# Order of a unit's maxima and the scaling of the unit ahead of it on VectorE, in a forgetting-attention stage

## The chip, the core and the metric

The kernel runs on one core of a Trainium2 chip. A core has five engines with instruction streams of their own: TensorE (PE; its weight loads are listed as PEld), VectorE (DVE), ScalarE (ACT), GpSimd (POOL) and SyncE (SP, which here issues DMA transfers). Each works through its own stream in order and waits on semaphores that the others raise. The metric is the device time of one execution in microseconds.

## What is computed

Two layers over a residual stream of 512 tokens by 1024 features, in float32: dilated sliding-window attention, a gated convolutional FFN, then forgetting attention with shared keys and values, and another FFN. The change lies in the forgetting attention:

```python
def fox_mixer(xn, w_q, w_o, k, v, c):
    q = (xn @ w_q).reshape(B, T, B_HEADS, HEAD_DIM)
    c_t = c.transpose(0, 2, 1)
    scale = HEAD_DIM ** -0.5
    for i in range(T // BLK):
        q0, q1 = i * BLK, (i + 1) * BLK
        s = jnp.einsum('bqhd,bkhd->bhqk', q[:, q0:q1], k[:, :q1]).astype(jnp.float32) * scale
        s = s + (c_t[:, :, q0:q1, None] - c_t[:, :, None, :q1])
        causal = jnp.arange(q0, q1)[:, None] >= jnp.arange(q1)[None, :]
        s = jnp.where(causal, s, NEG)
        p = jax.nn.softmax(s, axis=-1).astype(v.dtype)
        outs.append(jnp.einsum('bhqk,bkhd->bqhd', p, v[:, :q1]))
    o = jnp.concatenate(outs, axis=1)
    return o.reshape(B, T, B_WIDTH) @ w_o
```

There are 16 heads of 64 features and four blocks of 128 queries; block i sees (i + 1) x 128 keys.

## The kernel before

The program is written out in order for each engine; a library adds the semaphores and hands out buffers from pools (`t4`: ten buffers of 4 KB a partition, shared by raw weights, biases, probabilities and the rows of the cumulative gate; `bank`: eight banks of PSUM). Matrix products are made of three PE passes over operands split into a high and a low part, so that a weight that arrives as float32 goes through a copy on ACT (`W.high`, L57) and a subtraction on DVE (`W.low`, L69). In heads 2 to 5 of the attention the low part is made in another way: ACT writes the negated high part (`W.minus`, L64) and a DMA issued by POOL adds the raw weight to it (`W.low_added`, L84).

"Head" below is a pair of heads, 0 to 7, that share the 128 partitions; "block" is one of the four query blocks. A unit is (head j, block i), 32 in all, and the loop at L1668 runs over n with unit n alive and three rounds of tail. In round n:

- at block 2, PE does a quarter of a query projection (`q_part`), the scores of blocks 2 and 3 of this head and of blocks 0 and 1 of the next one (`f_scores`, L1578, tile `s_ps`), and then the products with the values of the head before (`f_pv`, L1627, tile `o_ps`); at other blocks PE does a quarter of a projection alone, up to head 7. From unit (6,3) on PE also does parts of the output projection (`po.both`, tile `acc`).
- `f_norm` takes the unit before (n - 1): a reciprocal of the row sums (L1598) and, for each of the two heads, a scaling of the probabilities in place (L1600), on DVE.
- `f_exp` takes unit n: for each of the two heads a DVE instruction adds the bias to the scores, writes the sum and keeps the row's extreme (L1588, followed by a read of its accumulator into `nm`), and ACT takes the exponential with the row sum (L1590).
- `f_bias` lets POOL make the bias of unit n + 1: two scalings of the gate's rows (L1560) and a causal select (L1561).
- then, at their blocks, DVE's low part of the query (`q_low`, L1506, block 1), of a weight (L69, block 2 in heads 0 and 1 and in units from (6,2) on), and of the output of the head before (`f_out_low`, L1641, block 3).
- `f_transpose` takes unit n - 2: PE transposes its scaled probabilities (L1612, tile `pT_ps`) and ACT copies them out (L1614).
- at block 1 of heads 2 to 5 come `W.minus` and `W.low_added`; `q_high` (L1500) at block 0, `f_out_high` (L1637) behind the values, `W.high` at one block a head.

The values of a head need the copies of all four of its units; the scores need banks that earlier reductions and copies have released. After the loop come the rest of the output projection, a norm and the last FFN (tile `first` is its first product).

The two functions:

```python
def f_exp(j, i):
    ...
    for hh in range(2):
        dve.tensor_tensor_reduce(p[:, hh, :n], s[hh][:, :n], bias[:, hh, :n], -0.125, BIG, ALU.add, ALU.min,
                                 nm[:, hh:hh + 1])
        act.activation(p[:, hh, :n], p[:, hh, :n], AF.Exp, bias=nm[:, hh:hh + 1], scale=-1.0,
                       accum_out=ls[:, hh:hh + 1])

def f_norm(j, i):
    ...
    dve.reciprocal(rl, ls)
    for hh in range(2):
        dve.tensor_scalar(p[:, hh, :n], p[:, hh, :n], rl[:, hh:hh + 1], None, ALU.mult)
```

Of the kernel before, what the change touches and what calls it, by code (L numbers as in the profile page):

```python
# [103 lines left out]
def trunk_kernel(ctx, tc, x, norm_gains, w_qkv_a, w_o_a, w_q_b, w_o_b, kv_norm, w_kvf, b_f,  # L104
# [14 lines left out]
    def t4(shape, dt=F32, name="t4"):  # L119
        return p4.tile(shape, dt, tag="t4", name=name)  # L120
# [7 lines left out]
    def small(n, name):  # L128
        return sml.tile([128, n], F32, tag=name, name=name)
# [1346 lines left out]
    def load_ck(j):  # L1476
        t = t4([128, 2, T], name="ck")
        s = cd[2 * j:2 * j + 2, :]
        sp.dma_start(t, bass.AP(tensor=s.tensor, offset=s.offset, ap=[[0, 128], [T, 2], [1, T]]))
        cks[j] = t  # L1480
# [4 lines left out]
    def q_part(j, i):  # L1485

        if j >= 8:
            return
        if i == 0:
            qps[j] = (bank([128, T], name="q_ps"), [t.rearrange("p (k c) -> p k c", k=8) for t in W.get()])  # L1490
        o, (wh, wl) = qps[j]
        for kc in (2 * i, 2 * i + 1):
            bh, bl = xs(xTq, kc, ALL)
            mm3(o, wh[:, kc, :], wl[:, kc, :], bh, bl, kc == 0, kc == KD - 1)

    def q_high(j):
        if j >= 8:
            return
        qT[j] = t8([128, 2, T], F32R, name="qst")
        act.copy(qT[j][:, 0], qps[j][0])  # L1500

    def q_low(j):
        if j >= 8:
            return
        o, t = qps.pop(j)[0], qT[j]
        dve.tensor_tensor(t[:, 1], o, t[:, 0].bitcast(F32), ALU.subtract)  # L1506
# [48 lines left out]
    def f_bias(j, i):  # L1555
        n = (i + 1) * 128
        bias = t4([128, 2, T], name="bias")
        for hh in range(2):
            hd = 2 * j + hh
            pool.tensor_scalar(bias[:, hh, :n], cks[j][:, hh, :n], -1.0, cq[:, i, hd:hd + 1], ALU.mult, ALU.add)  # L1560
        pool.affine_select(bias[:, :, n - 128:n], bias[:, :, n - 128:n], pattern=[[0, 2], [-1, 128]],  # L1561
                           compare_op=ALU.is_ge, fill=NEG, base=0, channel_multiplier=1)
        bia[j, i] = bias
# [3 lines left out]
    def f_scores(j, blocks):  # L1567
        wide = blocks[0] >= 2
        if not wide:
            both = [bank([128, 2, 256], name="s_ps") for _ in range(2)]  # L1570
        k = kst[j // 2][:, j % 2]
        for i in blocks:
            nn = max(256, (i + 1) * 128)
            sc[j, i] = [bank([128, T], name="s_ps") for _ in range(2)] if wide else [o[:, i] for o in both]
            for qp, kp in ((0, 0), (0, 1), (1, 0)):
                for hh in range(2):
                    own = slice(64 * hh, 64 * hh + 64)
                    pe.matmul(sc[j, i][hh][:, :nn], qT[j][own, qp, i * 128:(i + 1) * 128], k[own, kp, :nn],  # L1578
                              start=qp + kp == 0, stop=qp == 1)

    def f_exp(j, i):
        n = (i + 1) * 128
        s = sc.pop((j, i))
        bias = bia.pop((j, i))
        p = t4([128, 2, T], name="prob")
        nm, ls = small(2, "nm"), small(2, "ls")
# [5 lines that stand above are left out]
        prob[j, i] = (p, ls)  # L1592

    def f_norm(j, i):
        n = (i + 1) * 128
        p, ls = prob[j, i]
        rl = small(2, "rl")
# [3 lines that stand above are left out]
# [3 lines left out]
    def f_transpose(j, i):  # L1604
        p, _ = prob.pop((j, i))
        for hh in range(2):
            if i >= 2 or hh == 0:
                o = bank([128, 4, 128], name="pT_ps")
                t = t2([128, 4, 128], name="pT")
            k0 = (i + 1) * hh if i < 2 else 0  # L1610
            for k in range(i + 1):
                pe.transpose(o[:, k0 + k, :], p[:, hh, k * 128:(k + 1) * 128], ident)  # L1612
            if i >= 2 or hh == 1:
                act.copy(t[:, :k0 + i + 1], o[:, :k0 + i + 1])  # L1614
            pT[j, i, hh] = t[:, k0:k0 + i + 1]
# [4 lines left out]
    def f_pv(j, i):  # L1620
        if i == 0:
            ops[j] = bank([128, T], name="o_ps")
        o = ops[j]
        for k in range(i + 1):
            for hh in range(2):
                hd = 2 * j + hh
                pe.matmul(o[64 * hh:64 * hh + 64, i * 128:(i + 1) * 128],  # L1627
                          Vt[hd // 8][:, k, (hd % 8) * 64:(hd % 8) * 64 + 64], pT[j, i, hh][:, k, :],
                          start=k == 0, stop=k == i)
        del pT[j, i, 0], pT[j, i, 1]  # L1630

    def f_out_high(j):
        o = ops[j]
        if j % 2 == 0:
            OTb[j // 2] = t8([128, 2, 2, T], F32R, name=f"OTb{j // 2}")
        t = OTb[j // 2]
        act.copy(t[:, 0, j % 2, :], o)  # L1637

    def f_out_low(j):
        o, t = ops.pop(j), OTb[j // 2]  # L1640
        dve.tensor_tensor(t[:, 1, j % 2, :], o, t[:, 0, j % 2, :].bitcast(F32), ALU.subtract)  # L1641
# [16 lines left out]
    def values_of(n):  # L1658
        nonlocal pv_next
        while pv_next < n - 2:  # L1660
            j, i = units[pv_next]
            pv_next += 1
            f_pv(j, i)
            if i == 3:
                outs.append(j)

    f_scores(0, (0, 1))
    for n in range(N + 3):  # L1668
        live = n < N
        if live:  # L1670
            j, i = units[n]
            if i == 0 and j + 1 < 8:
                load_ck(j + 1)
            if i == 2:
                q_part(j + 2, 1)
                f_scores(j, (2, 3))
                if j + 1 < 8:
                    f_scores(j + 1, (0, 1))
                values_of(n)
        if 1 <= n <= N:  # L1680
            f_norm(*units[n - 1])
        if live:
            f_exp(j, i)
            if n + 1 < N:
                f_bias(*units[n + 1])
            if i == 1:
                q_low(j + 1)
            if i == 2 and j < 2 or (j, i) >= (6, 2):
                W.low()
            if i == 3 and j:  # L1690
                f_out_low(j - 1)
            if i != 2:
                q_part(j + 1 + (i > 0), (i + 3) % 4)
            if (j, i) in ((7, 1), (7, 2)):
                next(down1)
        if 2 <= n < N + 2:
            f_transpose(*units[n - 2])
        if live and i == 1 and 2 <= j < 6:
            W.minus()
            W.low_added()  # L1700
        if n >= N + 3 - len(fill):
            po.both(*fill[n - N - 3 + len(fill)])

        if n >= N and n % 4 in (0, 2):
            values_of(n)
        while outs:
            f_out_high(outs.pop())
        if live and i == 0:
            q_high(j + 1)
        if live and (i == (j < 2) if j < 6 else (j, i) >= (6, 1) and W.n_split < wo + 4):  # L1710
            W.high()
# [53 lines left out]
```

## Time and profile before

| what | value |
|---|---|
| median of 3 runs | 1111.93 us (1111.66 to 1112.12) |
| profiled execution, its own time | 1113.65 us |
| its span, first to last instruction | 1111.9 us |
| granted TensorE clock, mean | 0.999 |
| attention loop in the span | about 624 to 732 us |
| DVE, scalings L1600, in all | x64, 30.1 us, mean 511 ns |
| DVE, reductions L1588, in all | x64, 28.5 us, mean 481 ns |
| ACT, exponentials L1590, in all | x64, 35.6 us, mean 561 ns |

The profile is of one execution. A row of the order of time has the start in the span, the duration, engine, line, operation, output and inputs, shapes, the number of instructions merged, and in brackets the idle time just before it with what ended it. In "x2" rows the duration is that of both from the first's start to the second's end; neighbouring instructions overlap a little. Rows of waits read: who waited, for whom, microseconds in total, times, longest. A releaser is inferred from semaphores; where the named engine had long been done, it was another.

### The profile page before, as it was taken

The numbers are of one execution on the slowest core, as the hardware profiler recorded it, in microseconds if no ns is written. First come the engines' busy times: TensorE is split into PE (matmuls) and PEld (weight loads), VectorE is DVE, ScalarE is ACT, GpSimd is POOL, SyncE is SP. The second block draws the span as 40 slices with busy tenths as digits, with TensorE's granted clock in tenths as the row PEclk, the third lists the DMA queues.
The fourth block names the chain that finished last, engine by engine and source line by source line (L and its number), as shares of the span: only waits on it lengthen the run. The fifth ranks groups of instructions, "written<-read, shape, count | busy, mean of one in ns | idle before, by whom it ended". The sixth has DMA issues, their size and how long they took to land. (4 is left out here: it accounts for less than half of the span.)

```text
span 1111.9 us, 18030 instructions
## 1 busy us (share of the span) xinstructions
PE 1100.4 (99%) x6610; PEld 953.5 (86%) x6610; DVE 879.9 (79%) x1484; ACT 660.9 (59%) x1088; POOL 214.0 (19%) x313
## 2 busy tenths in 40 slices
PE   9999999999999999999999999999999999999997
PEld 5988889999999988888878888789999999988886
DVE  6597778888788779997686676868887887779994
ACT  5554566656666747576451487746556665747572
POOL 1823000411111211000000445500411111211000
PEclk9999999999999999999999999999999999999999
DMA  9499864368878989794448444593379788989872
GB/s 324 164 328 408 337 190 126 85 180 200 202 184 189 239 269 326 292 321 115 133 152 280 158 113 115 176 283 112 83 179 213 188 190 193 231 263 319 317 246 76
DMA packets 184242, 236.26 MB, mean 212 GB/s; under 512 B 11673, under 2 KB 131465, under 8 KB 184154
## 3 DMA queue, kind: packets, MB, share of 16 engines
q1 hardware_dynamic: 169210, 182.94, 50.2%
q0 software_dynamic: 14944, 52.18, 20.5%
q8 instruction: 52, 0.85, 0.3%
q14 instruction: 36, 0.29, 0.1%
HBM read 166.08 MB, written 39.63 MB: 185 GB/s over the span
## 5 line engine op out<-in xcount | busy, mean ns | idle before, releaser
L264 PE MATMUL acc<-w 128*128 128x512 f32 (+1 forms) x311 | 120.6, 388 | 0.3 <-DVE mix L326 0.3
L266 PE MATMUL acc<-w 128*128 128x512 f32 (+1 forms) x311 | 120.4, 387 | 0.0
L69 DVE TENSOR_TENSOR w<-wraw,w 128x1024 fp32r<-128x1024 f32 x74 | 97.4, 1332 | 25.6 <-ACT w L57 25.0
L57 ACT CAST w<-wraw 128x1024 fp32r<-128x1024 f32 x94 | 96.8, 1049 | 21.0 <-PE v_ps L265 6.9
L265 PE MATMUL acc<-w 128*128 128x512 f32 (+1 forms) x267 | 103.2, 387 | 0.0
L264 PE MATMUL up<-xsh,w 128*128 128x256 f32 x352 | 99.6, 283 | 0.0
L265 PE MATMUL up<-xsl,w 128*128 128x256 f32 x352 | 99.6, 283 | 0.0
L266 PE MATMUL up<-xsh,w 128*128 128x256 f32 x352 | 99.6, 283 | 0.0
L614 ACT ACTIVATE bb<-up,conv 128x512 f32<-128x512 f32 x80 | 59.6, 775 | 58.4 <-DVE up L1001 47.6
L265 PE MATMUL up<-xbl,w 128*128 128x512 f32 (+1 forms) x276 | 93.5, 339 | 0.0
L265 PE MATMUL up<-xcl,w 128*128 128x512 f32 (+1 forms) x276 | 93.5, 339 | 0.0
L264 PE MATMUL up<-xbh,w 128*128 128x512 f32 (+1 forms) x276 | 93.5, 339 | 0.0
L264 PE MATMUL up<-xch,w 128*128 128x512 f32 (+1 forms) x276 | 93.5, 339 | 0.0
L266 PE MATMUL up<-xbh,w 128*128 128x512 f32 (+1 forms) x276 | 93.4, 338 | 0.0
L266 PE MATMUL up<-xch,w 128*128 128x512 f32 (+1 forms) x276 | 93.4, 338 | 0.0
L264 PEld LDWEIGHTS acc<-w 128*128 128x128 f32 x311 | 58.4, 188 | 12.5 <-DVE mix L326 0.7
L266 PEld LDWEIGHTS acc<-w 128*128 128x128 f32 x311 | 58.4, 188 | 12.0
L264 PEld LDWEIGHTS up<-xsh,w 128*128 128x128 f32 x352 | 67.6, 192 | 0.0
L265 PEld LDWEIGHTS up<-xsl,w 128*128 128x128 f32 x352 | 67.6, 192 | 0.0
L266 PEld LDWEIGHTS up<-xsh,w 128*128 128x128 f32 x352 | 67.6, 192 | 0.0
L615 DVE SCALAR_TENSOR_TENSOR bb<-up,conv,bb 128x511 f32<-128x511 f32 x80 | 59.5, 744 | 5.5 <-ACT bb L614 5.2
L617 DVE SCALAR_TENSOR_TENSOR bb<-up,conv,bb 128x510 f32<-128x510 f32 x80 | 59.9, 749 | 2.8
(313 smaller groups left out, 3123.4 us busy)
## 6 DMA issues: line engine op xcount, KB each, us to landing
wraw<-in_w_up_dram SPq DMA_DIRECT2D x88, 512.0 KB, 6.0
w<-wraw POOLq DMA_DIRECT2D x32, 512.0 KB, 6.3
dT<-dsums SPq DMA_DIRECT2D x28, 512.0 KB, 7.6
w<-wsum POOLq DMA_DIRECT2D x24, 512.0 KB, 5.8
dsums<-in_w_down_dram SPq DMA_DIRECT2D x22, 512.0 KB, 7.6
dsums<-in_w_down_dram SPq DMA_DIRECT2D x44, 256.0 KB, 5.6
hD<-hc POOLq DMA_DIRECT2D x44, 256.0 KB, 6.5
dact<-hD SPq DMA_DIRECT2D x44, 256.0 KB, 5.9
```

Source lines behind the costliest of these rows:

```text
L57: self.nc.scalar.copy(pair[:, 0], raw)
L69: self.nc.vector.tensor_tensor(pair[:, 1], raw, pair[:, 0].bitcast(F32), ALU.subtract)
L264: pe.matmul(o, ah, bh, start=first, stop=False, skip_group_check=shared)
L265: pe.matmul(o, ah, bl, start=False, stop=False, skip_group_check=shared)
L266: pe.matmul(o, al, bh, start=False, stop=last, skip_group_check=shared)
L614: act.activation(bb[:, s, :], ps, AF.Identity, bias=cp[:, 3, ch:ch + 1], scale=cp[:, 2, ch:ch + 1])
L615: dve.scalar_tensor_tensor(bb[:, s, 1:], ps[:, :T - 1], cp[:, 1, ch:ch + 1], bb[:, s, 1:], ALU.mult, ALU.add)
L617: dve.scalar_tensor_tensor(bb[:, s, 2:], ps[:, :T - 2], cp[:, 0, ch:ch + 1], bb[:, s, 2:], ALU.mult, ALU.add)
```

## The change

In each round `f_exp` of the unit alive now comes ahead of `f_norm` of the unit before. Nothing else moves: `f_bias` and what follows keep their places, and in the last rounds, where no unit is alive, `f_norm` stands as it did.

```diff
                 if j + 1 < 8:
                     f_scores(j + 1, (0, 1))
                 values_of(n)
+        if live:
+            f_exp(j, i)
         if 1 <= n <= N:
             f_norm(*units[n - 1])
         if live:
-            f_exp(j, i)
             if n + 1 < N:
                 f_bias(*units[n + 1])
             if i == 1:
```

On DVE the order of one round was: reciprocal and two scalings of unit n - 1, two reductions of unit n. It becomes: two reductions of unit n, reciprocal and two scalings of unit n - 1. ACT's, POOL's, SP's and PE's streams keep their instructions and their order.

## The prediction

> **What bounds the kernel now.** I read the page's busy times first, then TensorE's (PE's) own waits in the attention stage from 618 to 735 us, then the order of time on PE, VectorE (DVE), ScalarE (ACT) and GpSimd (POOL) in that stage.
>
> ```profile
> PE 1100.4 (99%) x6610; PEld 953.5 (86%) x6610; DVE 879.9 (79%) x1484; ACT 660.9 (59%) x1088; POOL 214.0 (19%) x313
> ...
> PE s_ps L1578 <- ACT pT L1614: 1.0, 3, 0.5
> PE pT_ps L1612 <- DVE prob L1600: 0.5, 2, 0.3
> PE acc L264 <- DVE nm L1588: 0.4, 1, 0.4
> PE s_ps L1578 <- DVE nm L1588: 0.3, 1, 0.3
> ```
>
> PE is busy 99% of the span, so the kernel can gain only what PE still waits. The waits listed, with the 0.29 at 717.53 further down, are 2.5 us, all in the stage that the change touches, and all on DVE's reductions and scalings or on ACT's copies behind them. They understate the loss, because PE's row goes on for a while after its last real issue. The scores of a head against the values of the head before it show it better: both blocks have the same work for heads 2 to 6, and each scores block runs until the o_ps block starts.
>
> ```profile
> 652.41 2.21 PE L1578 MATMUL s_ps<-kst,qst 64*128 64x384 f32 x24
> 654.55 2.40 PE L1627 MATMUL o_ps<-pT,Vt 128*64 128x128 f32 x40
> ...
> 664.81 2.42 PE L1578 MATMUL s_ps<-kst,qst 64*128 64x384 f32 x24
> 667.16 2.40 PE L1627 MATMUL o_ps<-pT,Vt 128*64 128x128 f32 x40
> ...
> 677.38 1.61 PE L1578 MATMUL s_ps<-kst,qst 64*128 64x384 f32 x13
> ...
> 680.14 2.40 PE L1627 MATMUL o_ps<-pT,Vt 128*64 128x128 f32 x40
> ...
> 690.37 1.60 PE L1578 MATMUL s_ps<-kst,qst 64*128 64x384 f32 x13
> ...
> 693.09 2.40 PE L1627 MATMUL o_ps<-pT,Vt 128*64 128x128 f32 x40
> ...
> 700.03 1.29 PE L1612 MATMUL pT_ps<-ident,prob 128*128 128x128 f32 x8 [0.27 <-DVE prob L1600]
> 701.25 0.44 PE L1578 MATMUL s_ps<-kst,qst 64*128 64x384 f32 x1
> ...
> 705.20 2.40 PE L1627 MATMUL o_ps<-pT,Vt 128*64 128x128 f32 x40
> ...
> 712.67 1.25 PE L1612 MATMUL pT_ps<-ident,prob 128*128 128x128 f32 x8 [0.22 <-DVE prob L1600]
> ...
> 715.24 2.00 PE L1578 MATMUL s_ps<-kst,qst 64*128 64x384 f32 x12
> 717.53 2.40 PE L1627 MATMUL o_ps<-pT,Vt 128*64 128x128 f32 x40 [0.29 <-ACT pT L1614]
> ```
>
> Start to start, the scores take 2.14 us for head 2 (654.55 - 652.41), then 2.35, 2.76, 2.72 and 3.95 for heads 3 to 6. Against head 2 that is 0.21, 0.62, 0.58 and 1.81 lost. Head 7 has 12 of the 24 matmuls and takes 2.29; the wide half of 2.14 is about 1.3, so about 1.0 is lost. With the idle of the other waits on DVE (0.27 + 0.22 + 0.4) the loss is 5.1 us, my ceiling for what this stage can give. From head 2 to head 3 PE needs 12.40 us (664.81 - 652.41); later heads take 12.57 and 12.99. The loss grows from head to head: something beside PE is a little slower than PE and falls behind.
>
> That something is a ring through four engines. One turn, head 4 to head 5:
>
> ```profile
> 679.55 1.08 ACT L64 ACTIVATE w<-wraw 128x1024 fp32r<-128x1024 f32 x1
> ...
> 680.92 0.89 POOL L84 DMA_DIRECT2D w<-wraw  x1 [4.34 <-ACT w L64]
> ...
> 681.54 1.67 POOL L1560 TENSOR_SCALAR bias<-ck,cq 128x512 f32<-128x512 f32 x2
> ...
> 682.05 1.86 DVE L1600 TENSOR_SCALAR prob<-prob,rl 128x384 f32<-128x384 f32 x2
> ...
> 683.29 0.41 POOL L1561 TENSOR_SCALAR_AFFINE_SELECT bias<-bias 128x256 f32<-128x256 f32 x1
> ...
> 683.83 0.68 DVE L1588 CUSTOM_DVE_ANT_0 prob<-s_ps,bias 128x512 f32<-128x512 f32 x1
> ...
> 685.05 0.68 DVE L1641 TENSOR_TENSOR OTb<-o_ps,OTb 128x512 fp32r<-128x512 f32 x1
> ...
> 686.11 0.17 DVE L1598 RECIPROCAL rl<-ls 128x2 f32<-128x2 f32 x1 [0.37 <-ACT prob L1590]
> ...
> 686.31 1.02 DVE L1600 TENSOR_SCALAR prob<-prob,rl 128x512 f32<-128x512 f32 x2
> 687.25 0.28 DVE L1588 CUSTOM_DVE_ANT_0 prob<-s_ps,bias 128x128 f32<-128x128 f32 x1
> ...
> 687.62 0.40 ACT L1590 ACTIVATE prob<-prob,nm 128x128 f32<-128x128 f32 x1 [1.08 <-DVE nm L1588]
> ...
> 692.50 1.08 ACT L64 ACTIVATE w<-wraw 128x1024 fp32r<-128x1024 f32 x1
> ```
>
> ACT's negated weight (L64) releases POOL's accumulating DMA; behind that in POOL's order comes the bias of block 3, which the reduction of block 3 needs; then DVE's low part of the output (L1641), the exponential of block 3 awaited, its scaling, the reduction of the next head's block 0; then ACT's exponential, copies, a weight, and L64 again. In steps: 1.37 + 0.62 + 2.29 (681.54 to 683.83) + 1.22 + 2.20 (685.05 to 687.25) + 0.37 + 4.88 (687.62 to 692.50) = 12.95. PE needs 12.40. The ring loses 0.55 a head until PE waits for it.
>
> **The change part by part.** It removes and adds no instruction. In each of 31 units the two reductions (L1588, with their accumulator reads) and, on ACT, the two exponentials come ahead of the reciprocal and two scalings (L1598, L1600) of the unit before. No DMA is issued by either step; only DVE's order changes, and POOL, SP, ACT and PE keep theirs. So DVE's busy time stays, but three things change on the ring.
>
> First, the wait for the exponential goes. Today the step of 2.20 holds that wait and the scaling of block 3; afterwards the reduction of the next block 0 follows L1641 without either. What comes into the ring is the scaling of block 2, today done beside POOL's bias, afterwards queued behind the reduction of block 3, which waits for that bias. Its price has two ends:
>
> ```profile
> 636.47 0.88 DVE L1600 TENSOR_SCALAR prob<-prob,rl 128x512 f32<-128x512 f32 x2
> ...
> 640.02 1.36 POOL L1560 TENSOR_SCALAR bias<-ck,cq 128x512 f32<-128x512 f32 x2 [3.96 <-DVE nm L1588]
> ...
> 644.27 0.75 DVE L1600 TENSOR_SCALAR prob<-prob,rl 128x384 f32<-128x384 f32 x2
> ...
> 648.72 0.40 ACT L1590 ACTIVATE prob<-prob,nm 128x128 f32<-128x128 f32 x1 [0.99 <-ACT pT L1614]
> ...
> 685.23 0.94 POOL L1560 TENSOR_SCALAR bias<-ck,cq 128x256 f32<-128x256 f32 x2 [0.25 <-DVE nm L1588]
> ```
>
> Alone the two scalings of 384 take 0.75; beside POOL's bias of 512 they took 1.86, that is 1.11 more. In the new place POOL works on the bias of 256 (0.47 a piece), which starts as soon as the reduction of block 3 is done, just when the scaling starts. The nearest row for one blocked piece is the 1.11 beside pieces of 0.83; by size that is 0.63, so I take 1.38, between 0.75 and 1.86. The ring's 2.20 becomes 0.20 (reciprocal, 686.11 to 686.31) + 0.75 to 1.86 + 0.62 (L1641) = 1.57 to 2.68, taken 2.20: the same. Second, the bias of block 3 no longer runs beside a scaling: 1.36 for 1.67, 0.31 less. So a turn takes 12.0 to 13.1, taken 12.6: 0.2 a head behind PE in place of 0.55.
>
> Third, the ring starts earlier. The row at 648.72 shows ACT idle for 0.99 before the first exponential of head 2, waiting (the releaser named was long done) for the reduction that stood behind a scaling; that goes. The start of L64 after the first score of its head is 2.17 for head 4 (679.55 - 677.38); head 2 is two turns of about 0.5 earlier, 1.2. Afterwards 0.2 for head 2 and 0.2 more a head, 0.8 at head 5. Head 2 loses nothing at 1.2, head 3 0.21 at 1.7; so heads 3 to 5 lose nothing: 0.21 + 0.62 + 0.58 = 1.41 gained.
>
> What is late next is the scaling itself. It was ahead of the reduction and is now behind it, so PE's transposes of that unit (one unit later in PE's order) may wait.
>
> ```profile
> 662.46 1.04 PE L1612 MATMUL pT_ps<-ident,prob 128*128 128x128 f32 x8
> ```
>
> For blocks 0 to 2 a projection step or the values (2.4) lie between; hidden. Block 3 is scaled after the next head's first reduction: 1.37 + 0.62 + 1.98 + 1.22 + 2.20 = 7.4 after L64 that reduction starts, two halves take 0.4, the reciprocal 0.2, and the first half of the scaling 0.44 (0.88 / 2) alone or 1.0 behind a blocked piece of 0.6; taken 8.8. PE gets there 10.1 after the first score of an undisturbed head (662.46 - 652.41), and with L64 0.2 to 0.6 after that score the scaling is through at 9.0 to 9.4: hidden. In head 5 PE has no projection step left to put between and gets there at 8.8 (700.03 - 0.27 - 690.37 - 0.58); the scaling is through at 0.8 + 8.8 = 9.6, so PE waits 0.8 where it waits 0.27 now: 0.5 lost. If the cover went in every head, it would be rival (c).
>
> Head 6: scores wait today for copies and reductions that the ring delivers late (1.81). With the ring 1.4 earlier against PE, the last copy of head 5 ends before the values want it: 1.8 gained. Heads 6 and 7 then load DVE with three low parts of weights. Between the first reduction of (6,2) and the scaling of (6,3) DVE then also does the scaling of (6,1), 0.2 + 0.5 (two thirds of 0.75), and the reduction of (7,0), 0.4: 1.1 more. It starts earlier by what the ring has gained on PE, 1.3 at head 5 (2.13 to 0.8), of which head 5's longer wait at its transposes takes back 0.5: net 0.3 later. Waits of 0.4 + 0.22 become about 0.8 to 0.9: 0.2 lost. By head 7's scores this DVE work is through, and the copy that PE waits for there has no idle ACT before it: 1.0 gained.
>
> Sum: 1.4 + 1.8 + 1.0 - 0.5 - 0.2 = 3.5, and 0.3 for the earlier start of what comes after a wait (the idle of 0.27, 0.22 and 0.4 leaves out PE's refill): 3.8 us. The profiled execution took 1113.65 with a span of 1111.9, so 1.75 lies around the span; it would take 1109.85. The runs shown have a median of 1111.93, so 1108.1.
>
> Does the gain survive to the end?
>
> ```profile
> 745.20 1.05 ACT L57 CAST w<-wraw 128x1024 fp32r<-128x1024 f32 x1 [0.85 <-DMA wraw<-in_w_up_dram]
> ...
> 766.68 0.28 PE L264 MATMUL first<-xch,w 128*128 128x256 f32 x1
> ...
> PE acc L264 <- DVE mix L326: 0.3, 1, 0.3
> ```
>
> The fourth up-weight of the last FFN has its high part at 746.3, 20 us before the first product; and from 735 us to the end PE waits once, 0.3 us. PE simply arrives earlier.
>
> By the Trainium skill, page "SBUF — State Buffer", section "Who interferes with whom", a DVE instruction in a two-port mode and a GpSimd instruction exclude each other for the whole instruction, and whichever starts first wins. The rows agree (1.86 beside POOL, 0.75 alone). This speaks against the change, since each reduction now releases a bias on POOL at the moment that a scaling starts; it is the first rival.
>
> **The rivals.** (a) Every scaling that meets a bias waits for a whole piece each time: 0.47 twice for block 2, so the ring is 12.0 + 0.94 = 12.9, as slow as today, and only the head start of 1.0 is left: L64 comes 0.2, 0.7, 1.3 and 1.8 after the first score of heads 2 to 5, and head 5 loses 0.3 in its scores. Block 3's scaling meets the bias of 384 (a piece lies between 0.47 for 256 and 0.68 for 512, say 0.58), and its first half is through 9.3 after L64, so at 9.5, 10.0, 10.6 and 11.1 against 10.1 and, in head 5, 8.8: PE waits 0.5 in head 4 and, the ring having gained on PE by these 0.8, 1.5 in head 5. From 3.8 come off 0.3 + 0.5 + 0.7 (1.5 for 0.8): 2.3 gained, 1109.6. For it: 1.86. Against it: the scaling at 686.31 ran beside POOL's work and took 1.02 against 0.88 alone.
>
> (b) The change does not do what it says: the waits of PE go but others of the same size stand behind them (buffers freed by transposes that are now later, DMA in the last stage), 1111.9. For it: the ring's other steps (12.95 - 2.20) are untouched. Against it: the 20 us above.
>
> (c) Slower: the scaling becomes the slow member. Its place is between the reduction of block 3 and PE's transposes; its price is the full 1.86 in the ring, 13.1 a turn, and 0.2 for the landing of the accumulating DMA, whose raw weight's buffer the next probabilities take. PE is then paced at 13.3 instead of 12.40, 12.57 and 12.99: 39.9 - 38.0 = 1.9 over three heads and 0.5 in head 5, 2.4 in all: 1114.3. It decides from a ring of 12.7 (38.0 / 3) on, once the head start of 1.0 is used up. Against it: 12.6 is my middle. For it: each full block costs 1.1 a head.
>
> **How the numbers follow.** Chances: forecast 0.62, (a) 0.18, (b) 0.11, (c) 0.09. What a measurement can tell from no change is about 0.2%, 2.2 us: below 1109.7 is faster, above 1114.1 slower. Faster: 0.62 x 0.97 + half of (a), which lies on the bound = 0.69; slower 0.08, most of (c); the rest, 0.23, is within. The range reaches down to the ceiling with refill, 5.1 + 0.6 = 5.7 gained, 1106.2, and up past (a) to the lower edge of (b), 1111.7, which leaves out (c) and half of (b). The forecast's own range is 1106.2 to 1109.5.
>
> **What would show it.** On DVE each L1588 pair stands before L1598, and ACT's idle before block 0's exponential (1.08, 0.99) is gone. The scores of heads 3 to 6 take about 2.14 up to the o_ps row. PE's waits on L1600 stay or grow at the transposes of (5,3) and (6,3); waits on L1614 vanish. L64 comes every 12.4 to 12.6 us. The prediction is wrong if L1600 beside POOL takes 1.9 in the new place as a rule, if PE waits on prob L1600 in heads 2 to 4, or if new waits arise after 735 us.

## The result, and the profile after

The changed kernel takes 1110.51 us (median of 15 runs, 1109.56 to 1111.58) beside 1112.24 for the kernel before (15 runs): a ratio of 0.9982, 95% interval 0.9974 to 0.999, so 1.1 to 2.9 us less. A second comparison (E9 below) gave 0.9979, 0.9969 to 0.999. The forecast was 1108.1, a gain of 3.8, in a range from 1106.2 to 1111.7. The gains of the two comparisons, 1.7 and 2.7 us, lie near rival (a)'s 2.3; the time is inside the range, but above the forecast's own 1106.2 to 1109.5.

The two profiled executions differ by more, 1113.65 and 1109.58, but not all of that is the change. PE's clock on five rows of the order of time, before and after, columns as in the prediction:

```profile
624.62 0.97 PE L1578 MATMUL s_ps<-kst,qst 64*128 64x256 f32 x12
...
642.16 2.40 PE L1627 MATMUL o_ps<-pT,Vt 128*64 128x128 f32 x40
...
730.08 1.75 PE L1627 MATMUL o_ps<-pT,Vt 128*64 128x128 f32 x28
```

```profile
623.16 0.98 PE L1578 MATMUL s_ps<-kst,qst 64*128 64x256 f32 x12
...
641.31 2.40 PE L1627 MATMUL o_ps<-pT,Vt 128*64 128x128 f32 x40
...
651.56 2.21 PE L1578 MATMUL s_ps<-kst,qst 64*128 64x384 f32 x24
653.71 2.40 PE L1627 MATMUL o_ps<-pT,Vt 128*64 128x128 f32 x40
...
688.67 2.21 PE L1578 MATMUL s_ps<-kst,qst 64*128 64x384 f32 x24
690.82 2.40 PE L1627 MATMUL o_ps<-pT,Vt 128*64 128x128 f32 x40
...
697.65 1.29 PE L1612 MATMUL pT_ps<-ident,prob 128*128 128x128 f32 x8 [0.16 <-ACT prob L1590]
698.87 2.62 PE L1578 MATMUL s_ps<-kst,qst 64*128 64x384 f32 x24
701.42 2.40 PE L1627 MATMUL o_ps<-pT,Vt 128*64 128x128 f32 x40
...
709.14 0.66 PE L1612 MATMUL pT_ps<-ident,prob 128*128 128x128 f32 x4 [1.08 <-DVE prob L1600]
...
712.02 1.49 PE L1578 MATMUL s_ps<-kst,qst 64*128 64x384 f32 x12
713.44 2.40 PE L1627 MATMUL o_ps<-pT,Vt 128*64 128x128 f32 x40
...
725.98 1.75 PE L1627 MATMUL o_ps<-pT,Vt 128*64 128x128 f32 x28
```

PE is 1.46 us earlier at the first score already, ahead of the first changed instruction; that belongs to the start of the program in that one execution of before, where PE waits 1.0 and 0.3 us (`qk_ps`) that it does not wait after. In the fourteen profiles of this document the first score lies between 622.97 and 624.62. From the first score (first row) to the last values (last row) the stage takes 105.5 us before and 102.8 after, 2.6 less, which lies inside the intervals of the runs. This stage time is the measure used below. What lies behind it is 381.8 us in both, and there PE's one wait is the one of before (`acc <- DVE mix`, 0.3): nothing is given back later. It is 381.8 in the other runs too, but for E6 (382.3) and E7 (382.0), where a weight load of the last FFN waits 0.7 and 0.4 for a landing.

PE's waits after, all of the stage (who, for whom, us, times, longest):

```profile
PE pT_ps L1612 <- DVE prob L1600: 1.5, 3, 1.1
...
PE pT_ps L1612 <- ACT pT L1614: 0.3, 1, 0.3
PE pT_ps L1612 <- ACT prob L1590: 0.2, 1, 0.2
```

The waits of the scores on copies (1.0) and those on the reductions (0.4 and 0.3) are gone, and PE now waits longer for scalings, 1.5 for 0.5. The same ring as in the prediction, head 4 to head 5, after:

```profile
677.03 1.08 ACT L64 ACTIVATE w<-wraw 128x1024 fp32r<-128x1024 f32 x1
...
678.41 0.89 POOL L84 DMA_DIRECT2D w<-wraw  x1 [3.96 <-ACT w L64]
678.42 2.44 DVE L1600 TENSOR_SCALAR prob<-prob,rl 128x256 f32<-128x256 f32 x2
...
679.03 1.67 POOL L1560 TENSOR_SCALAR bias<-ck,cq 128x512 f32<-128x512 f32 x2
...
681.22 0.69 DVE L1588 CUSTOM_DVE_ANT_0 prob<-s_ps,bias 128x512 f32<-128x512 f32 x1 [0.36 <-POOL bias L1561]
...
682.63 1.25 POOL L1560 TENSOR_SCALAR bias<-ck,cq 128x256 f32<-128x256 f32 x2 [0.25 <-DVE rl L1598]
...
682.64 0.90 DVE L1600 TENSOR_SCALAR prob<-prob,rl 128x384 f32<-128x384 f32 x2
...
683.47 0.67 DVE L1641 TENSOR_TENSOR OTb<-o_ps,OTb 128x512 fp32r<-128x512 f32 x1
...
684.06 0.28 DVE L1588 CUSTOM_DVE_ANT_0 prob<-s_ps,bias 128x128 f32<-128x128 f32 x1
...
684.43 0.41 ACT L1590 ACTIVATE prob<-prob,nm 128x128 f32<-128x128 f32 x1 [0.41 <-DVE nm L1588]
...
689.32 1.09 ACT L64 ACTIVATE w<-wraw 128x1024 fp32r<-128x1024 f32 x1
```

A turn is 12.29 us here, 12.95 before. ACT's idle ahead of block 0's exponential is 0.41, 1.08 before. The scaling of block 2 stands in the ring now and takes 0.90; beside it POOL's pieces for 256 keys take 1.25 where they took 0.94.

### The profile page after: what moved, and what is told of

It is laid out like the page before. It is cut to its first block, busy times and chain, and to the rows that moved or that the text cites. A ratio compares the mean times of both kernels' runs of the same rounds, so it can differ in the third digit from the quotient of the medians.

```text
span 1107.8 us, 18033 instructions
## 1 busy us (share of the span) xinstructions
PE 1097.9 (99%) x6610; PEld 952.7 (86%) x6610; DVE 880.1 (79%) x1484; ACT 661.2 (60%) x1088; POOL 218.8 (20%) x313
## 4 chain that ended last, share of the span: by engine, by line
PE 94%; DVE 2%; ACT 2%; DMA 1%; issue 1%; POOL 0%; DVEq 0%; ACTq 0%; POOLq 0%
PE up L266 13%; PE up L265 13%; PE up L264 13%; PE acc L264 8%; PE acc L266 8%; PE acc L265 8%; PE v_ps L264 2%; PE v_ps L266 2%; PE v_ps L265 2%; PE qk_ps L265 2%; PE qk_ps L264 2%; PE qk_ps L266 2%; PE first L264 1%; PE first L266 1%; PE first L265 1%; PE k_ps L264 1%
```

## The experiments

All runs at a glance; "stage" is from the profile of the run, worked out from unrounded times. The medians of before beside them are 1112.58 (E1 to E4), 1113.11 (E5 to E8) and 1112.5 (E9 to E12).

| run | order of maxima and scaling | median us | ratio to before, 95% | stage us |
|---|---|---|---|---|
| before | old | 1112.24 | | 105.47 |
| changed | new | 1110.51 | 0.9982, 0.9974 to 0.999 | 102.81 |
| E1 | new at block 0 alone | 1109.65 | 0.9974, 0.9962 to 0.9985 | 103.25 |
| E2 | new at block 3 alone | 1113.86 | 1.001, 1.0001 to 1.002 | 106.53 |
| E3 | old in round 3 | 1109.76 | 0.9975, 0.9965 to 0.9984 | 103.45 |
| E4 | old in round 28 | 1108.93 | 0.9973, 0.9963 to 0.9984 | 102.25 |
| E5 | old in rounds 3 and 28 | 1109.98 | 0.9972, 0.9962 to 0.9982 | 101.69 |
| E6 | new, buffers exchanged | 1109.55 | 0.9971, 0.996 to 0.9982 | 102.45 |
| E7 | E5, buffers exchanged | 1108.77 | 0.9961, 0.9948 to 0.9974 | 101.57 |
| E8 | new at block 0, not 28, buffers exchanged | 1109.06 | 0.9967, 0.9955 to 0.9979 | 101.56 |
| E9 | the changed kernel again | 1109.81 | 0.9979, 0.9969 to 0.999 | 102.80 |
| E10 | old, buffers exchanged | 1112.89 | 1.0, 0.9992 to 1.0009 | 105.57 |
| E11 | E8, L1641 of head 5 later | 1109.15 | 0.9969, 0.9957 to 0.9981 | 101.93 |
| E12 | new up to round 8, not 3 | 1111.98 | 0.9993, 0.9984 to 1.0002 | 105.18 |

The intervals are 2 to 3 us wide, so they part most kernels from before and hardly from each other, and the changed kernel's own median moved by 0.7 from one comparison to the other; between variants the stage and the rows decide. Each stage is that of one execution: E9 repeats the changed kernel's within 0.01, but E3 and E5, which are the same up to round 28, are 1.15 apart by head 5's values (78.90 and 77.75 from the first score).

All variants of the order use one form of the edit, with another condition:

```diff
-        if live:
-            f_exp(j, i)
+        first = live and (i == 0)
+        if first:
+            f_exp(j, i)
         if 1 <= n <= N:
             f_norm(*units[n - 1])
         if live:
+            if not first:
+                f_exp(j, i)
```

### Which swap makes the gain: E1, E2, E12

E1 has this condition.

> The maxima come first only where a head's block 0 is alive (rounds 4, 8, ... 28); elsewhere the order is that of before. Ring theory (the gain comes from the one step of 2.20 us in the ring, in which DVE waits for the exponential of block 3 and scales it ahead of the next head's first reduction): that step becomes 0.62 (L1641 alone), nothing is added to the ring, so a turn is 12.95 - 2.20 + 0.62 = 11.4 us of its own, below PE's 12.4. PE sets the pace: scores blocks of heads 2 to 5 at 2.14 us and 12.4 apart as in the changed kernel, the whole gain of heads 3 to 6 is there, and the 0.85 us which the changed kernel loses at the transposes of unit (0,2) are not lost, since round 3 has the old order; the wait at the transposes of (6,3), about 1 us, stays. So 0.5 to 1 us below the changed kernel, 1109.5 to 1110 for its 1110.5, 2 to 2.7 below before. Rival (each of the swaps gives a share, because any earlier reduction frees banks and starts exponentials earlier): 7 or 8 of 31 swaps give about a quarter of the 1.7 us, 1111.8, with scores of heads 4 and 5 at 2.5 us.

```diff
+        first = live and (i == 3)
```

> The maxima come first only where block 3 is alive. Ring theory: the wait for the exponential and the scaling of block 3 stay in the ring, the scaling of block 2 comes into it behind the reduction of block 3 (0.20 + 0.75 to 1.86; 0.90 beside POOL in the changed kernel), and only 0.31 comes off the bias: a turn of 12.95 + 0.8 = 13.7 us, from 13.6 to 14.7. From head 3 on PE is paced by it: scores of heads 4 to 6 start 13 to 13.8 apart, and the kernel is slower than before by 2 to 3.5 us, 1114 to 1116. Rival (any swap gives a share): a quarter of 1.7, 1111.8, scores 12.6 apart. Rival (the head start alone counts): the same as before, 1112.

```diff
+        first = live and (n <= 8 and n != 3)
```

> The new order in rounds 1, 2 and 4 to 8 alone (heads 0 and 1 and the first block of head 2), the old one from there on; no exchange of buffers. It has the earlier start of the ring and the old turn of 12.95. Theory (both the start and the turn count): L64 comes 0.2 us after the first score in head 2 and 0.55 later in each head, 1.8 at head 5, so heads 3 and 4 lose nothing and head 5 0.2 to 0.3; from there on waits as before. About 1.2 of the 1.4 us of heads 3 to 5 are gained, and part of head 6's: stage 103.3 to 104.2. Rival (the turn alone counts): stage 105 or more. Rival (the start alone counts): stage 102 to 102.8, no worse than the whole change.

The swap at block 0 alone brings the gain (0.9974), the one at block 3 alone is slower (1.001, an interval that just leaves out 1, and a stage 1.1 longer), and the early rounds alone bring next to nothing (stage 0.3 shorter, as the first rival of E12 had it). The signs are those of the ring theory. Blocks 1 and 2 alone were not tried. In E2, order of time, ACT:

```profile
652.85 1.08 ACT L64 ACTIVATE w<-wraw 128x1024 fp32r<-128x1024 f32 x1
...
666.14 1.08 ACT L64 ACTIVATE w<-wraw 128x1024 fp32r<-128x1024 f32 x1
...
679.43 1.08 ACT L64 ACTIVATE w<-wraw 128x1024 fp32r<-128x1024 f32 x1
...
692.71 1.08 ACT L64 ACTIVATE w<-wraw 128x1024 fp32r<-128x1024 f32 x1
```

Every turn is 13.3, not the 13.7 expected (13.6 to 14.7): the scaling added to the ring covers the wait for the exponential (0.37 before) that was in it; in E2 the reciprocal at 686.47 follows L1641 without a wait. The head start, a term of the prediction, is worth little by itself. E12 had L64 0.26 after the first score of head 2, as expected, but its first turn with the old order took 13.27, because an early ring meets PE:

```profile
656.31 0.37 ACT L1614 COPY pT<-pT_ps 128x256 f32<-128x256 f32 x1 [2.09 <-PE pT_ps L1612]
...
657.05 0.73 ACT L1590 ACTIVATE prob<-prob,nm 128x512 f32<-128x512 f32 x1
...
659.99 0.41 ACT L1590 ACTIVATE prob<-prob,nm 128x128 f32<-128x128 f32 x1 [0.93 <-ACT pT L1614]
```

ACT waits 2.09 for PE's transposes, so the exponential of block 3 is late, and in the old order DVE, and ACT's next exponential (0.93), wait for it again.

E1 has the time that was expected, but not for the reason given: its stage is 0.4 longer than the changed kernel's, not shorter, and its turn, which should have been 11.4 of its own, was 13.81 behind head 4 (676.31 to 690.12). In heads 3 and 4 DVE stood still (order of time, DVE):

```profile
671.04 0.29 DVE L1588 CUSTOM_DVE_ANT_0 prob<-s_ps,bias 128x128 f32<-128x128 f32 x1 [1.38 <-DMA w<-wraw]
...
681.82 0.68 DVE L1641 TENSOR_TENSOR OTb<-o_ps,OTb 128x512 fp32r<-128x512 f32 x1
684.85 0.29 DVE L1588 CUSTOM_DVE_ANT_0 prob<-s_ps,bias 128x128 f32<-128x128 f32 x1 [2.35 <-issue]
```

The reduction of the next head's block 0 writes probabilities into the buffer of the raw weight that POOL's accumulating DMA still reads. The first row names that DMA, which landed at 670.92. The second names none, but the DMA of head 4, issued at 677.69, took 7.04, and the reduction starts 0.12 after its landing, as in head 3. The DMA is a second branch of the ring, from L84 straight to that reduction. The prediction's sum did not have it; rival (c) alone named it, at 0.2.

### Where the gain is lost: E3, E4, E5, E9

```diff
+        first = live and (n != 3)
```

> The changed kernel with the old order in round 3 alone, so unit (0,2) is scaled ahead of the reductions of (0,3). Theory: the wait of PE at the transposes of (0,2) (0.17 + 0.20 in its row and more in refill, 0.85 us in its clock against before) goes, and since the ring of heads 2 to 6 is not touched, all of it stays to the end: 0.85 below the changed kernel, 1109.7. Rival (head 0's delay is taken up by PE's slack against the ring, which is then met earlier): no change, 1110.5, scores of heads 3 to 6 above 2.14.

```diff
+        first = live and (n != 28)
```

> The changed kernel with the old order in round 28 alone, so unit (6,3) is scaled ahead of the reductions of (7,0). Theory: the wait of PE at the transposes of (6,3) (1.08 + 0.27 in the changed kernel, 0.22 before) shrinks by the 0.4 to 0.7 us of the reductions that go behind it: 0.5 us below the changed kernel, 1110.0, with about 0.5 of the wait left because DVE's low weights stand ahead of it too. Rival (the wait is caused by the weight's low part alone, which waits for ACT): wait still 1 us, 1110.5. Rival (moved reductions delay the exponentials of (7,0) and with them the end of the loop): wait gone, but the time is the same, lost again at head 7's scores.

```diff
+        first = live and (n not in (3, 28))
```

> The changed kernel with the old order in rounds 3 and 28 both. Landing theory, from the traces of the first four: in heads 3 and 4 the reduction of the next head's block 0 waits for the landing of POOL's accumulating DMA (L84), since its probabilities take the raw weight's buffer; the DMA takes 4.8 to 7.0 us, longer when the row of the gate and a raw weight are on their way too. So the 0.85 us that PE saves in head 0 are lost again at heads 4 and 5, as in the run without round 3 alone (0.99 waited at the transposes of (5,3)), and the time is that of the run without round 28, 1108.9, within 0.4. Rival (the two losses are independent): 1108.9 - 0.85 = 1108.1, no wait at the transposes of (5,3) over 0.3.

E9 has no edit.

> The changed kernel once more, beside the three below and the kernel before on the same chip. From the first comparison 1.7 us below before, from the stage of the profiles (102.81 us from the first score to the last values, before 105.47) 2.7; theory: the stage in this profile is 102.5 to 103.5, with the same waits at the transposes of (0,2) (0.17 and 0.20) and (6,3) (1.0 to 1.1).

E4 came as expected: stage 0.56 shorter, wait 0.60 in place of 1.08 + 0.27. E3 did not. The two waits in head 0 went, but only 0.35 us of PE's time by head 0's values (17.80 from the first score, 18.15 in the changed kernel, 17.54 before; the loss was 0.61, not the 0.85 of the expectation), and PE then waited 0.99 at the transposes of (5,3). In E3 the landings of heads 3 and 4 took 6.42 and 6.16, in the changed kernel 6.06 and 5.33, and the turns behind them 13.20 and 12.93 for 12.85 and 12.29. In E5 the same code up to round 28 had 5.94 and 5.39 and kept its gain, against the expectation: stage 0.56 below E4. So the loss in E3 was of that execution. The medians do not show the gain of E5: 1109.98 is above the expected 1108.9 and the rival's 1108.1, and its ratio (0.9972) is about E4's (0.9973).

The rest of head 0's loss does not come from round 3. Where rounds 1 and 2 are swapped and round 3 is not (E3, E12), PE is 0.4 late behind the transposes of (0,3) instead: the projection behind them starts 14.12 and 14.14 after the first score, in E1 and before 13.71. The scalings that now stand behind the reductions have moved DVE's later work back; the scaling of (0,3) starts 12.55 after the first score in E3, 11.86 in E1. Where round 3 is swapped and rounds 1 and 2 are not (E2), nothing is lost by head 0's values (17.41; E1 17.39).

### Taking the landing out of the ring: E6, E7, E8, E10

```diff
+        ahead = live and i == 0 and 3 <= j <= 6
+        if ahead:
+            f_bias(*units[n + 1])
         first = live and (True)
...
-            if n + 1 < N:
+            if n + 1 < N and not ahead:
                 f_bias(*units[n + 1])
```

The order on each engine stays; only the buffers of the two tiles change hands.

> The changed kernel with the buffers of two tiles exchanged in heads 3 to 6: POOL's bias of block 1 is set up ahead of the probabilities of block 0, so the bias takes the raw weight's buffer and waits for the landing, and the probabilities take the buffer of the bias of block 3. No instruction is added or moved on an engine. Landing theory: the step from L84 to the reduction of the next block 0, 5.65 us in head 4 of the changed kernel and 6.1 in head 3, falls to what DVE needs; turns of L64 are 12.4 or less in all heads (one was 12.85), the scores of head 6 take 2.2 instead of 2.55 us: 0.4 below the changed kernel, 1110.1. Rival (the wait moves on: the bias of block 1 is now late, and the reduction of block 1 with its exponentials, which ACT does ahead of L64 too, waits as long): turns as before, 1110.5, and a DVE wait for POOL's bias ahead of the 128x256 reductions.

The condition of E5 with it:

> Both edits together: old order in rounds 3 and 28, and the exchange of buffers. Landing theory: with the landing out of the ring the 0.85 us of head 0 stay to the end, the transposes of (5,3) wait less than 0.4, and the time is about 1.0 below the kernel with rounds 3 and 28 alone: 1107.8. Rival (the wait moves to the bias of block 1): the same as rounds 3 and 28 alone, 1108.9.

`i == 0 and j < 7` with it:

> The new order at block 0 alone, heads 1 to 6, old order elsewhere (round 28 too), with the exchange of buffers. Ring theory: nothing but DVE's own order bounds a turn, 11.4 us, so PE paces all heads at 12.4: L64 within 0.3 us of the first score in heads 2 to 5, no 0.8 us lost at the transposes of (4,3) and before the values of head 4 as in the run with block 0 alone: 1109.65 less 0.8 less 0.6 for round 28: 1108.2 or a little below. Rival (landing matters only by chance of other transfers, not through this buffer): 1109.0, with the 0.8 still lost.

The old order with it:

> The old order everywhere, with the exchange of buffers alone. Ring theory: in the old order the reduction of the next block 0 stands behind the wait for the exponential and the scaling of block 3, 0.33 us after the landing in head 4 (686.92 and 687.25), so the landing bounds little: the same as before within 0.5 us, stage 105.0 to 105.5, L64 12.9 to 13.0 apart. Rival (the exchange by itself brings the gain of the later kernels): 1.5 us or more below before.

In the changed kernel and in E6, the reduction of block 0 behind head 3 and who waits for the landing (order of time, DVE and POOL; E6 is the second):

```profile
670.67 0.67 DVE L1641 TENSOR_TENSOR OTb<-o_ps,OTb 128x512 fp32r<-128x512 f32 x1
671.75 0.29 DVE L1588 CUSTOM_DVE_ANT_0 prob<-s_ps,bias 128x128 f32<-128x128 f32 x1 [0.41 <-POOL bias L1561]
```

```profile
670.95 0.28 DVE L1588 CUSTOM_DVE_ANT_0 prob<-s_ps,bias 128x128 f32<-128x128 f32 x1
...
671.74 1.27 POOL L1560 TENSOR_SCALAR bias<-ck,cq 128x256 f32<-128x256 f32 x2 [2.32 <-DMA w<-wraw]
...
682.04 0.75 DVE L1600 TENSOR_SCALAR prob<-prob,rl 128x384 f32<-128x384 f32 x2
```

In the first the 0.41 is put down to POOL's bias, which had long been done; the DMA landed at 671.63. In E6 POOL waits for the landing instead, and the scaling of block 2 runs alone, in 0.75. L64 comes every 12.43, 12.38 and 12.37 us, where the changed kernel has 12.38, 12.85 and 12.29, and the stage is 0.36 shorter, as expected; but head 6's scores, where it was expected, still take 2.63; the gain lies ahead of them, where PE goes from head 5's scores to head 6's in 9.67 us (688.47 to 698.14) instead of 10.20 (688.67 to 698.87). E7 and E8 reach 101.57 and 101.56; in them no instruction of DVE waits for a landing, and E8's L64 stays within 0.3 of the first score, as expected. E7's stage is only 0.12 below that of E5, whose landings were short; E8's is 1.7 below E1's, 0.56 of which round 28 is worth by E4. Their medians, 1108.77 and 1109.06, miss the 1107.8 and 1108.2 expected and are nearer to the rivals' 1108.9 and 1109.0, so that the landing's part rests on the rows. E10 shows no gain from the exchange in the old order (turns 12.83 to 13.24): the landing binds only once the order is changed.

E7 has the lowest median of all, 0.9961 of before, though its interval reaches into those of the others.

### A try beyond: E11

```diff
+            if n == 28:
+                f_out_low(5)
...
-            if i == 3 and j:
+            if i == 3 and j and n != 27:
                 f_out_low(j - 1)
```

> As the run with block 0 alone and the exchange of buffers, not round 28, and with the low part of head 5's output (L1641) behind the scaling of (6,3) instead of ahead of it. Theory: the scaling is 0.6 us earlier on DVE, so the wait at the transposes of (6,3), 0.42, is gone, and the stage is 0.4 to 0.6 shorter, 101.0 to 101.2; time 1108.3, the best of all. Rival (DVE waits ahead of that for the weight's high part on ACT, so nothing moves; or the bank that is freed later makes PE wait elsewhere): stage 101.5 as before.

A miss: the stage is 0.37 longer than E8's, for the second reason that its rival gave (order of time, PE):

```profile
707.34 0.63 PE L1612 MATMUL pT_ps<-ident,prob 128*128 128x128 f32 x4
709.00 0.66 PE L1612 MATMUL pT_ps<-ident,prob 128*128 128x128 f32 x4 [1.03 <-DVE OTb L1641]
```

The first half of the transposes no longer waits for the scaling; the second needs the bank that L1641 releases, and L1641 is now later.

## Why the prediction was right in its mechanism and short in its size

PE's gain over before, by stretch, from the rows of both profiles:

| stretch | foreseen | measured |
|---|---|---|
| first score to head 0's values | 0 | -0.61 |
| to head 4's values | 1.41 | 1.42 (0.85 to 2.27) |
| to head 5's values: scores of head 6 and transposes of (5,3) | 1.8 - 0.5 | 1.51 (2.27 to 3.78) |
| to the last values | 1.0 - 0.2 | 0.32 (3.78 to 4.10) |
| PE's start-up behind a wait (the prediction's refill) | 0.3 | in the above |
| sum | 3.8 | 2.64 |

- **The ceiling and the reading of the loss** held: the scores of heads 2 to 5 take 2.15 (653.71 - 651.56, 690.82 - 688.67), and from head 0's values to head 4's PE gains 1.42 for 1.41. The last 0.3 of the sum, PE's refill, has no row of its own in any run; a lag of that kind is seen at (0,2), where the listed idle is 0.17 + 0.20 and PE comes out 0.77 later.
- **The ring** held in length: L64 comes 0.24 after the first score in head 2 (foreseen 0.2) and 0.65 in head 5 (0.8), turns 12.29 to 12.85 (12.6 taken). Its terms did not. The scaling of block 2 took 0.90, not 1.38, with POOL's pieces longer beside it (0.94 became 1.25). The bias of block 3 still took 1.67, not 1.36, and the prediction's reason, a scaling beside it, was wrong: in E2 DVE is idle from 680.4 to 683.6, and the bias takes 1.67 all the same (POOL and DVE below). In heads 4 and 5 it follows POOL's DMA issue at once and takes 1.64 to 1.69 in every run; at 640.02, without an issue ahead, it took 1.36. And the landing, no term of the sum, set the turn of 12.85. The head start of 1.0 and the shorter turn do not add up as two terms, as E12 shows.

```profile
680.81 0.89 POOL L84 DMA_DIRECT2D w<-wraw  x1 [4.34 <-ACT w L64]
681.43 1.67 POOL L1560 TENSOR_SCALAR bias<-ck,cq 128x512 f32<-128x512 f32 x2
...
683.62 0.69 DVE L1588 CUSTOM_DVE_ANT_0 prob<-s_ps,bias 128x512 f32<-128x512 f32 x1 [3.23 <-POOL bias L1561]
```

- **The step that failed** is "For blocks 0 to 2 a projection step or the values (2.4) lie between; hidden". It fails in head 0. There no values lie between, and DVE makes a weight's low part (1.22) between the scaling of (0,1) and the reductions of (0,3). PE comes out of the transposes of (0,2) 0.77 later than before (635.37 - 623.16 for 636.06 - 624.62). In head 1 the same low part stands there (641.81), but the values lie between, and PE does not wait. DVE, and then PE, in the changed kernel:

```profile
630.46 0.61 DVE L1600 TENSOR_SCALAR prob<-prob,rl 128x256 f32<-128x256 f32 x2
630.99 1.22 DVE L69 TENSOR_TENSOR w<-wraw,w 128x1024 fp32r<-128x1024 f32 x1
632.12 0.69 DVE L1588 CUSTOM_DVE_ANT_0 prob<-s_ps,bias 128x512 f32<-128x512 f32 x1
...
633.54 1.41 DVE L1600 TENSOR_SCALAR prob<-prob,rl 128x384 f32<-128x384 f32 x2
```

```profile
634.34 0.55 PE L1612 MATMUL pT_ps<-ident,prob 128*128 128x128 f32 x3 [0.17 <-DVE prob L1600]
...
635.09 0.52 PE L1612 MATMUL pT_ps<-ident,prob 128*128 128x128 f32 x3 [0.20 <-DVE prob L1600]
```

- **(6,3) was mis-sized**: waits of "about 0.8 to 0.9" were 1.08 + 0.27, and head 7's 1.0 was 0.87 (2.29 before, 1.42 after). Again a scaling was blocked, and again a weight's low part stands ahead of it (DVE, changed kernel): 1.49 in place of 0.88. In E4 it comes 0.42 earlier, at 708.01, and takes 1.14.

```profile
706.08 1.23 DVE L69 TENSOR_TENSOR w<-wraw,w 128x1024 fp32r<-128x1024 f32 x1 [0.46 <-ACT w L57]
...
708.43 1.49 DVE L1600 TENSOR_SCALAR prob<-prob,rl 128x512 f32<-128x512 f32 x2
```

- **(5,3) and head 6**: the wait of 0.8 at (5,3) was 0.16 (697.65), and 0.99 in E3, whose landing came later; head 6's scores take 2.55, 0.4 above the others, so 1.4 of the 1.8 came.
- **Rival (a)** holds in places, not as a rule: 0.90 in the ring, but 1.41 at (0,2) and 1.49 at (6,3). The measured gain is near its 2.3, but not by its path: in head 4 PE does not wait, and L64 in head 5 is at 0.65, not 1.8. **Rival (c)** did not come. E2 has its 13.3 a turn, but by luck: the scaling of block 2 takes 0.90 there (685.05), not 1.86, and the rest is the scaling of block 3, which stays in that ring. **Rival (b)** did not come as it was put: PE's listed waits in the stage are still 2.0 of 2.5, but the stage is 2.6 shorter, and nothing arose after 735 us.

By the Trainium skill, page "SBUF — State Buffer", section "Who interferes with whom", whichever of a two-port DVE instruction and a GpSimd instruction issues first has the ports and the other blocks. The rows at 682.63 and 682.64 (POOL 0.31 longer, DVE 0.15 longer than its 0.75 in E6) and at 678.42 (DVE 2.44) agree that either can be the one that waits. They do not show that the first to start wins: at 682.63 POOL's row starts 0.01 ahead of DVE's, and POOL's is the one that grows more.

## What to carry to other kernels

Of a swap on an in-order engine, ask at each place which of the two results is awaited first: here block 0 alone earns the gain, block 3 alone costs, and in two places, head 0 and round 28, where other work stands ahead of the moved step, about 0.6 us is lost each time. A cover worked out for the steady state has to be worked out again for the first and last turns. When a step is made earlier, look for what else releases it: a buffer handed on by a DMA can be the next bound, and giving that buffer to a tile that is needed later takes it out without an instruction moved. Whether the 0.5 and 0.2 that E6 and E7 lose behind the stage have to do with that is open; E8, E10 and E11, with the same exchange, lose nothing there.

## What the runs showed of the hardware

The accumulating DMA of one raw weight (512 KB) lands 4.76 to 4.93 us after issue in head 5, in all profiles, where a row of the gate alone is issued behind it, and 5.28 to 7.04 in head 4, where such a row is issued 2.3 us and a raw weight 2.8 to 3.3 us behind it. In head 4 the eight profiles with the weight at 2.86 or later have 5.28 to 5.43, the six with it at 2.83 have 5.92 to 7.04. Head 3 does not follow that: with the weight 2.85 behind it took 4.80 before, with 3.25 or more 5.79 to 6.42 (ten profiles). Whether the other transfers cause any of this wasn't tried.

One pair of scalings of 256 keys took 2.44 beside POOL's DMA issue and both pieces of a bias (678.42 to 680.86), 0.61 alone (630.46). Its second piece ends 0.15 after POOL's second, at 680.71, so it sat through several POOL instructions in a row, not one.
